# Weight pieces stored as they are loaded, with 4096-byte runs, and split by one operation of 1024 columns

## The chip, the cores and the metric

The kernel runs on one core of one Trainium2 chip. The metric is the device time of one execution in microseconds (us). A core has TensorE (matrix products, PE in the profile), VectorE (DVE), ScalarE (ACT), GpSimd (POOL) and SyncE (SP), each with its own instruction queue that is worked off in order, and 16 DMA engines that move data between HBM and the on-chip memory (SBUF) for whichever engine issued the transfer.

## The reference

One layer of a streaming encoder, for 1024 prompt rows and 64 sample rows that share the weights. All data are fp32, and D is 1024.

```python
xn = rmsnorm(x, g_mix)
p = xn @ w_in + b_in                      # 1024 -> 9224 columns: q, k, v, ig, fg, og, su, sv, xq, gates
h_a = sigmoid(og) * norm(mlstm(q, k, v, ig, log_sigmoid(fg)))
h_b = gelu(su) * (w_s @ rmsnorm(gelu(sv)) + b_s)
h_c = softmax(xq @ mem_k.T / 16) @ mem_v  # mem_k, mem_v = rmsnorm(mem) @ w_mk, w_mv
x = x + (g0 * h_a + g1 * h_b + g2 * h_c) @ w_out
# PEER: 8 heads, 128 x 128 product keys, the best 16 of 16384 experts for each row and head
q = rmsnorm(x, g_ffn) @ w_pq
e, g = top16(q @ k_sub1, q @ k_sub2)
x = x + sum_k g[k] * gelu(u_exp[e[k]] . xn) * v_exp[e[k]]
y = rmsnorm(x, g_final)
```

## The kernel before

The rows are nine tiles of up to 128 rows, in three blocks: [0, 1], [2, 3, 4, "s"] and [5, 6, 7]. "s" is the sample.

**Weights.** All dense weights pass through one stream of 560 pieces of 512 KB, each an SBUF tile of 128 partitions x 1024 columns. The list `pieces` holds them in the order of use: pieces 0 to 15 are w_mk and w_mv, then come 96 for each block (w_in, w_out, w_pq), and pieces 304 to 559 are the experts' matrices for the dense path. In DRAM a piece of a dense weight is two rows of 512 columns for each partition (runs of 2048 bytes), one of u_exp_t four rows of 256 columns (1024 bytes), one of v_exp two rows of 512 (2048 bytes). `w_load` issues a piece on SyncE into one of three buffers `wraw`; in the second phase every fourth piece goes to a further buffer, `wrawx`.

**Splits.** TensorE works in fp32r, and each weight is split in two parts: ScalarE casts a half of a piece (512 columns) to `wh` (line 277), and VectorE subtracts `wh` from it, which gives `wl` (line 280). For halves 192 to 223, GpSimd does the subtraction. Each half thus has its own pair of tiles, of which there are four (`HL`). The products with a half are the three terms xh*wh, xh*wl and xl*wh, in lines 311 to 313, 328 to 330, 1109 to 1111 and 1258 to 1260. The user of half i calls `w_get`, which first writes out the splits up to half i + 3, so the split of half i + 3 goes to the tiles of half i - 1 and waits until TensorE is done with those.

**Experts.** Tiles 0, 1, "s", 6 and 7 take their experts row by row: GpSimd issues an indirect DMA for each of 576 rows of u (tile `gu`, three buffers) and 576 rows of v (`gv`, four buffers), each of 128 x 4096 bytes (line 1018). VectorE consumes a u gather in line 1031 (a dot product with the row) and a v gather in line 1039 (a weighted sum into `gacc` or `gx`), one instruction of 128 x 1024 each. A buffer is gathered into again when VectorE is done with it.

**Dense path.** Tiles 2 to 5 take all 16384 experts as dense products, from piece 304 on: `hidden` (gelu of x times u, two pieces for 256 experts), times the expert weights that were spread out to `gd` in DRAM, and `dense` (times v, two pieces for 256 experts). A half is used by 12 matrix products of 512 columns here. `weigh` makes the two parts of a product with a cast (line 1228) and a subtraction (line 1229) of 1024 columns.

**Order.** Several generators (the blocks, mLSTM, the side branches, retrieval, the choice of experts, the gathers, the dense path) yield estimated costs to `Flow`, which writes out next the one that is furthest behind. The program so written passes a scheduler that puts each engine's instructions in order by its own simulated times. An engine's queue is in order at run time, so a subtraction of a split that stands behind a gather's consumption on VectorE waits for that gather too.

## Time and profile before

| | |
|---|---|
| median of three runs | 3675.89 us (3674.61 to 3696.73) |
| the profiled execution | 3700.63 us, of which the span from the first to the last instruction is 3698.9 us |
| TensorE busy | 3280.4 us (89%), 15364 matrix products recorded |
| VectorE busy | 3102.7 us (84%) |
| ScalarE busy | 1367.2 us (37%) |
| GpSimd busy | 1721.0 us (47%) |
| DMA | 1024.78 MB, 277 GB/s on average |

Matrix products are pipelined, so that a busy TensorE says only that it always had one under way. GpSimd's busy time is that of issuing the gathers and of a few operations. A wait is put down to the instruction that released it last.

### The profile page before, as it was taken

Reading aid. Unit: us, or ns where it says so; the run is one execution under the profiler, and the core shown is the slowest. Engines: PE = TensorE matmul, PEld = TensorE weight load, DVE = VectorE, ACT = ScalarE, POOL = GpSimd, SP = SyncE. Lnnn points to the kernel's source line nnn. Section 1 sums busy time; section 2 is a strip of 40 time slices with the busy share of each in tenths; the row PEclk is TensorE's granted clock in tenths of the full one; section 3 lists DMA queues with packets and bytes.
Section 4 is the critical chain, followed back from the end, with each engine's and each line's share of the span. In section 5 each row is a group of like instructions: output and inputs, shape, how many; then the busy total and the mean of one; then the engine's idle time right before and its main releaser. Section 6 shows DMA issues by size and latency. Waiting matters only on the chain.

```text
span 3698.9 us, 46231 instructions
## 1 busy us (share of the span) xinstructions
PE 3280.4 (89%) x15364; PEld 2632.8 (71%) x15364; DVE 3102.7 (84%) x6492; ACT 1367.2 (37%) x2479; POOL 1721.0 (47%) x1208
## 2 busy tenths in 40 slices
PE   8999998889996595898939765998999999999998
PEld 7787876576675473776938664876678888888886
DVE  5556797768899999899998999887798888879984
ACT  5555533423333242333415653322233333333332
POOL 1001334447765775465333475444465555446540
PEclk9999999999998697998959767999999999999999
DMA  7556477788897887898867788888899999989982
GB/s 230 148 165 188 152 245 248 254 279 321 320 367 273 272 306 252 276 334 285 302 209 220 235 269 292 312 287 276 295 376 337 337 339 337 328 282 386 356 303 85
DMA packets 447436, 1024.78 MB, mean 277 GB/s; under 512 B 32182, under 2 KB 169566, under 8 KB 443100
## 3 DMA queue, kind: packets, MB, share of 16 engines
q0 software_dynamic: 166528, 604.58, 47.0%
q1 hardware_dynamic: 276828, 413.06, 33.6%
q10 hardware_dynamic: 3840, 4.20, 0.3%
q8 instruction: 120, 1.97, 0.2%
q14 instruction: 120, 0.98, 0.1%
HBM read 968.44 MB, written 53.26 MB: 276 GB/s over the span
## 4 chain that ended last, share of the span: by engine, by line
PE 46%; DVE 20%; issue 13%; DMA 11%; POOL 8%; ACT 1%; POOLq 0%; DVEq 0%; ACTq 0%; SPq 0%
DMA gu<-in_u_exp_dram,e 7%; POOL gu L1018 5%; PE po L1260 5%; PE po L1259 5%; PE po L1258 5%; PE ph L1109 4%; PE ph L1111 4%; PE ph L1110 4%; DVE gacc L1039 4%; DVE gu L1031 4%; PE acc L312 3%; PE acc L311 3%; PE acc L313 3%; DVE wl L280 2%; DMA gv<-in_v_exp_dram,e 2%
## 5 line engine op out<-in xcount | busy, mean ns | idle before, releaser
L1018 POOL DMA_INDIRECT gv<-in_v_exp_dram,e x522 | 842.1, 1613 | 671.9 <-DVE gacc L1039 294.9
L1018 POOL DMA_INDIRECT gu<-in_u_exp_dram,e x576 | 756.8, 1314 | 774.6 <-DVE gu L1031 491.2
L277 ACT CAST wh<-wraw 128x512 fp32r<-128x512 f32 x994 | 613.0, 622 | 1347.9 <-PE ph L1110 481.5
L1031 DVE SCALAR_TENSOR_TENSOR gu<-gu,gx 128x1024 f32<-128x1024 f32 x576 | 701.6, 1220 | 195.2 <-DMA gu<-in_u_exp_dram,e 192.7
L280 DVE TENSOR_TENSOR wl<-wraw,wh 128x512 fp32r<-128x512 f32 x962 | 655.0, 686 | 228.4 <-ACT wh L277 226.2
L1039 DVE SCALAR_TENSOR_TENSOR gacc<-gv,w,gacc 128x1024 f32<-128x1024 f32 x448 | 573.1, 1279 | 33.3 <-DMA gv<-in_v_exp_dram,e 32.8
L312 PE MATMUL acc<-wl,half 128*128 128x512 f32 (+1 forms) x1152 | 474.1, 412 | 4.1 <-DVE wl L280 4.1
L313 PE MATMUL acc<-wh,half 128*128 128x512 f32 (+1 forms) x1152 | 456.2, 402 | 0.0
L1258 PE MATMUL po<-wh,W 128*128 128x512 f32 x1024 | 403.2, 399 | 32.6 <-ACT W L1228 32.6
L1111 PE MATMUL ph<-dxh,wl 128*128 128x512 f32 x1024 | 403.0, 394 | 18.5 <-DVE wl L280 18.4
L311 PE MATMUL acc<-wh,half 128*128 128x512 f32 (+1 forms) x1152 | 412.0, 410 | 6.5 <-ACT uB L470 5.1
L1259 PE MATMUL po<-wl,W 128*128 128x512 f32 x1024 | 408.7, 399 | 7.9 <-DVE wl L280 7.8
L1260 PE MATMUL po<-wh,W 128*128 128x512 f32 x1024 | 407.6, 398 | 0.6 <-DVE W L1229 0.6
L1109 PE MATMUL ph<-dxh,wh 128*128 128x512 f32 x1024 | 401.5, 392 | 1.3 <-DVE dxl L1133 1.3
L1110 PE MATMUL ph<-dxl,wh 128*128 128x512 f32 x1024 | 400.9, 391 | 0.0
L328 PE MATMUL acc<-half,wh 128*128 128x256 f32 (+2 forms) x768 | 250.2, 346 | 17.8 <-ACT wh L277 13.1
L311 PEld LDWEIGHTS acc<-wh,half 128*128 128x128 f32 (+1 forms) x1152 | 210.3, 184 | 77.8 <-issue 15.1
L312 PEld LDWEIGHTS acc<-wl,half 128*128 128x128 f32 (+1 forms) x1152 | 211.7, 184 | 71.4 <-issue 12.5
L329 PE MATMUL acc<-half,wh 128*128 128x256 f32 (+2 forms) x768 | 258.9, 342 | 0.0
L1258 PEld LDWEIGHTS po<-wh,W 128*128 128x128 f32 x1024 | 194.0, 189 | 80.3 <-issue 33.7
L313 PEld LDWEIGHTS acc<-wh,half 128*128 128x128 f32 (+1 forms) x1152 | 210.7, 184 | 54.4 <-issue 1.9
L330 PE MATMUL acc<-half,wl 128*128 128x256 f32 (+2 forms) x768 | 228.4, 343 | 15.5 <-DVE wl L280 8.5
(446 smaller groups left out, 5062.1 us busy)
## 6 DMA issues: line engine op xcount, KB each, us to landing
wraw<-in_w_in_dram SPq DMA_DIRECT2D x216, 512.0 KB
wraw<-in_v_exp_dram SPq DMA_DIRECT2D x126, 512.0 KB
wraw<-in_u_exp_t_dram SPq DMA_DIRECT2D x67, 512.0 KB
gd<-sg SPq DMA_DIRECT2D x16, 2048.0 KB
g<-gd SPq DMA_DIRECT2D x32, 1024.0 KB
wrawx<-in_u_exp_t_dram SPq DMA_DIRECT2D x61, 512.0 KB
wraw<-in_w_pq_dram SPq DMA_DIRECT2D x48, 512.0 KB
wraw<-in_w_out_dram SPq DMA_DIRECT2D x24, 512.0 KB
```

The lines of the kernel that those rows point to most:

```text
L277: S.copy(h, t)
L280: E.tensor_tensor(l, t, h.bitcast(F32), op=ALU.subtract)
L311: T.matmul(ps[i], xh[:, cs], h, start=(k == 0), stop=False)
L312: T.matmul(ps[i], xh[:, cs], l, start=False, stop=False)
L313: T.matmul(ps[i], xl[:, cs], h, start=False, stop=(last and b is None))
L1018: G.indirect_dma_start(out=tl, out_offset=None, in_=src, in_offset=bass.IndirectOffsetOnAxis(ap=col, axis=0))
L1031: V.scalar_tensor_tensor(tl, tl, 1.0, xn, op0=ALU.mult, op1=ALU.mult, accum_out=av[:, j:j + 1])
L1039: V.scalar_tensor_tensor(x2, gt_.pop(op), st_v[t][1][:, j:j + 1], x2, op0=ALU.mult, op1=ALU.add)
L1111: T.matmul(o, l[:, cs], xh[:, k + kk, :], start=False, stop=(k + kk == KD - 1))
L1258: T.matmul(o, hi, h, start=(q == 0 and k == 0), stop=False)
L1259: T.matmul(o, hi, l, start=False, stop=False)
L1260: T.matmul(o, lo, h, start=False, stop=(q == GP - 1 and k == 1))
```

## The change

All dense weights are stored in DRAM as the pieces themselves: for each piece 128 partitions x 1024 columns, so that each partition's part is one run of 4096 bytes. The content of a piece in SBUF is what it was. The eight gate columns of w_in get an array of their own, with runs of 256 bytes in place of 32. Everything else in `_layout` stays.

`wh` and `wl` become tiles of 1024 columns, a whole piece, with two buffers each in place of four of 512: as many bytes as before. For pieces 0 to 119 a piece is still cast and subtracted in two operations of 512 columns; from piece 120 on (`W1`), it is one cast and one subtraction of 1024. `w_get` of half i writes out the splits up to piece i // 2 + 1. At the first half of piece p, both halves of piece p + 1 are split into the tiles of piece p - 1; at the second half nothing is written. Before, the first half of piece p + 1 was written one half earlier. The loads have the same number, size and buffers, and GpSimd takes the same pieces (96 to 111) in halves.

```diff
-    RAW, HL = 3, 4
+    RAW, HL = 3, 2
...
     def want(src, c0):
         for kp in range(4):
-            pieces.append(src[kp * 256:(kp + 1) * 256, c0:c0 + 512].rearrange("(k p) c -> p k c", p=128))
+            pieces.append(src[c0 // 512, kp])
...
     POOL = 192, 224
+    POOL = POOL[0] // 2, POOL[1] // 2
+    W1 = 120
...
-        SP.dma_start(t.rearrange("p (k c) -> p k c", k=src.shape[1]), src)
+        SP.dma_start(t, pieces[i])
...
     def w_split():
-        i = W["split"]
-        if i >= 2 * len(pieces):
+        p = W["split"]
+        if p >= len(pieces):
             return
-        p, kk = divmod(i, 2)
         while W["load"] <= p:
             w_load()
-        t = raw_t[p][:, kk * 512:(kk + 1) * 512]
-        h = wp.tile([128, 512], F32R, name="wh", bufs=HL)
-        l = wp.tile([128, 512], F32R, name="wl", bufs=HL)
-        S.copy(h, t)
-
-        E = G if POOL[0] <= i < POOL[1] else V
-        E.tensor_tensor(l, t, h.bitcast(F32), op=ALU.subtract)
-        split_t[i] = (h, l)
+        t = raw_t.pop(p)
+        h = wp.tile([128, D], F32R, name="wh", bufs=HL)
+        l = wp.tile([128, D], F32R, name="wl", bufs=HL)
+
+        E = G if POOL[0] <= p < POOL[1] else V
+
+        n = 512 if p < W1 else D
+        for c in range(0, D, n):
+            cs = slice(c, c + n)
+            S.copy(h[:, cs], t[:, cs])
+            E.tensor_tensor(l[:, cs], t[:, cs], h[:, cs].bitcast(F32), op=ALU.subtract)
+        for c in range(2):
+            split_t[2 * p + c] = h[:, c * 512:(c + 1) * 512], l[:, c * 512:(c + 1) * 512]
         W["split"] += 1
-        if kk == 1:
-            raw_t.pop(p)
-            w_load()
+        w_load()
...
     def w_get():
         i = W["got"]
-        while W["split"] <= min(i + HL - 1, 2 * len(pieces) - 1):
+        while W["split"] <= min(i // 2 + HL - 1, len(pieces) - 1):
             w_split()
...
-                pieces.append(a["u_exp_t"][r * 512:(r + 1) * 512, m * 256:(m + 1) * 256]
-                              .rearrange("(k p) e -> p k e", p=128))
+                pieces.append(a["u_exp_p"][m, r])
...
-            pieces.append(a["v_exp"][e0:e0 + 256, hf * 512:(hf + 1) * 512].rearrange("(k p) c -> p k c", p=128))
+            pieces.append(a["v_exp_p"][GP * g + q, hf])
...
+    def parts(m):
+
+        return c(m.reshape(4, 2, 128, -1, 512).transpose(3, 0, 2, 1, 4).reshape(-1, 4, 128, 1024))
```

The scheduler orders each engine's instructions anew. Three places on VectorE show what came of it. The first is where the splits change their size, pieces 121 and 122, while the experts of the first block are chosen (`oh`, `ei` are tiles of that choice). Before:

```order
L280 TENSOR_TENSOR wl<-wraw,wh 128x512
L883 SCALAR_TENSOR_TENSOR xy<-pq__4542,xy 128x128
L889 SCALAR_TENSOR_TENSOR oh<-xy,ib 128x256 x4
L280 TENSOR_TENSOR wl<-wraw,wh 128x512
L892 TENSOR_TENSOR oh<-oh 128x512
L894 TENSOR_TENSOR ei<-oh 128x256
```

Now:

```order
L284 TENSOR_TENSOR wl<-wraw,wh 128x1024
L894 TENSOR_TENSOR oh<-oh 128x512
L896 TENSOR_TENSOR ei<-oh 128x256
L891 SCALAR_TENSOR_TENSOR oh<-xy,ib 128x256 x4
L647 COPY gt<-ms 128x12
```

What stood between the two subtractions of a piece now stands behind the one. The second place is in the third block, pieces 263 and 264, where VectorE consumes gathers of u and v, chooses experts (`scv`, `pos`, `tk`) and splits. Before:

```order
L280 TENSOR_TENSOR wl<-wraw,wh 128x512 x2
L1031 SCALAR_TENSOR_TENSOR gu,av<-gu,gx 128x1024
L1039 SCALAR_TENSOR_TENSOR gacc<-gv,w_17058,gacc 128x1024
L199 TENSOR_SCALAR rs<-rs 128x4
L1031 SCALAR_TENSOR_TENSOR gu,av<-gu,gx 128x1024
L800 MAX_INDEX pos<-scv,cand 128x8
L801 MATCH_REPLACE tk<-scv,cand 128x54
```

Now:

```order
L284 TENSOR_TENSOR wl<-wraw,wh 128x1024
L1033 SCALAR_TENSOR_TENSOR gu,av<-gu,gx 128x1024
L1041 SCALAR_TENSOR_TENSOR gacc<-gv,w_16042,gacc 128x1024
L879 TENSOR_TENSOR xy<-pq__11704 128x128
L874 SCALAR_TENSOR_TENSOR pq__11704<-pq__11704 128x128
L877 SCALAR_TENSOR_TENSOR pq__11704<-pq__11704 128x128
L883 TENSOR_TENSOR xy<-pq__11704 128x128
L1033 SCALAR_TENSOR_TENSOR gu,av<-gu,gx 128x1024
```

The gathers stand alike about a piece here, and the choice of experts has come further by this piece (`xy` is a later step of it than `pos`). Counted over VectorE's whole order, 524 of the 1152 gathers are consumed ahead of the end of piece 304's split before, and 536 now; ahead of piece 320's, 638 and 642; of piece 384's, 777 and 786. The third place is on the dense path, pieces 431 and 432, where VectorE has little but splits and gathers left (`ge` is the product with the expert weights). Before:

```order
L280 TENSOR_TENSOR wl<-wraw,wh 128x512
L1039 SCALAR_TENSOR_TENSOR gacc<-gv,w_24766,gacc 128x1024
L280 TENSOR_TENSOR wl<-wraw,wh 128x512
L1031 SCALAR_TENSOR_TENSOR gu,av<-gu,gx 128x1024
L1093 TENSOR_TENSOR ge<-ge,g_23951 128x1024
L1039 SCALAR_TENSOR_TENSOR gacc<-gv,w_24766,gacc 128x1024
```

Now:

```order
L284 TENSOR_TENSOR wl<-wraw,wh 128x1024
L1095 TENSOR_TENSOR ge<-ge,g_22495 128x1024
L1041 SCALAR_TENSOR_TENSOR gacc<-gv,w_23238,gacc 128x1024
L1033 SCALAR_TENSOR_TENSOR gu,av<-gu,gx 128x1024
L1041 SCALAR_TENSOR_TENSOR gacc<-gv,w_23238,gacc 128x1024
```

A piece had one to three other instructions behind each half's subtraction, and has all of them in a row behind the whole piece's.

## Rows read from the trace of the kernel before

**Rows 1.** The view of stretches, seven of them from the first to the last instruction: microseconds, then the busy time of TensorE (PE), its weight loads (PEld), VectorE (DVE), ScalarE (ACT) and GpSimd (POOL) with the number of instructions, the granted share of TensorE's clock, the busy share of the 16 DMA engines, and GB/s.

```profile
0.00:470.00 470.00, 444.89 (x2359) 367.95 (x2360) 283.13 (x825) 262.37 (x501) 51.99 (x55) 0.99 0.57 175
470.00:1100.00 630.00, 582.10 (x2486) 418.20 (x2486) 518.31 (x1086) 215.03 (x443) 355.81 (x246) 0.96 0.85 291
1100.00:1900.00 800.00, 616.09 (x2798) 504.70 (x2796) 760.59 (x2192) 271.88 (x520) 446.01 (x301) 0.86 0.84 284
1900.00:2400.00 500.00, 379.17 (x2333) 327.90 (x2334) 469.33 (x1003) 230.49 (x436) 266.28 (x130) 0.80 0.80 260
2400.00:2700.00 300.00, 274.62 (x1137) 214.37 (x1136) 228.88 (x355) 81.05 (x121) 128.04 (x107) 0.98 0.85 290
2700.00:3590.00 890.00, 888.95 (x3854) 723.96 (x3853) 791.00 (x959) 276.84 (x406) 472.87 (x371) 1.00 0.95 342
3590.00:3698.00 108.00, 94.55 (x405) 75.68 (x403) 51.42 (x80) 29.58 (x53) 0.00 (x0) 0.96 0.29 100
```

**Rows 2.** The waits of VectorE in three stretches, 470 to 1100 (two rows), 2400 to 2700 (one) and 2700 to 3590 (two): total microseconds, times, longest.

```profile
DVE gu L1031 <- DMA gu<-in_u_exp_dram,e: 92.2, 67, 5.9
DVE gacc L1039 <- DMA gv<-in_v_exp_dram,e: 14.0, 8, 3.8
...
DVE gu L1031 <- DMA gu<-in_u_exp_dram,e: 69.0, 45, 5.3
...
DVE wl L280 <- ACT wh L277: 71.8, 93, 2.0
DVE gu L1031 <- DMA gu<-in_u_exp_dram,e: 10.7, 8, 2.6
```

**Rows 3.** The waits of TensorE from 1100 to 1900 (two rows), 2400 to 2700 (two) and 2700 to 3590 (one), columns as in rows 2.

```profile
PE ms L819 <- ACT sc L822: 67.3, 8, 16.4
PE ms L733 <- DVE bb L720: 23.6, 2, 18.3
...
PE ph L1111 <- DVE wl L280: 18.4, 16, 2.7
PE po L1259 <- DVE wl L280: 6.8, 8, 2.2
...
PE po L1259 <- DVE wl L280: 1.0, 1, 1.0
```

**Rows 4.** Groups of instructions by line and shape, in the stretches 470 to 1100 (one row), 1100 to 1900 (two), 1900 to 2400 (two), 2400 to 2700 (three) and 2700 to 3590 (four): out<-in, shapes, count, busy microseconds, mean nanoseconds of one, and the idle time in front of them with what ended it. L280 is the subtraction of a split and L277 its cast; L1229 and L1228 are a subtraction and a cast of 1024 columns that the kernel does elsewhere; L1039 and L1031 consume a gather.

```profile
L280 DVE TENSOR_TENSOR wl<-wraw,wh 128x512 fp32r<-128x512 f32 x160 | 108.5, 683 | 2.0 <-ACT wh L277 1.8
...
L1039 DVE SCALAR_TENSOR_TENSOR gacc<-gv,w,gacc 128x1024 f32<-128x1024 f32 x161 | 205.3, 1275 | 10.9 <-DMA gv<-in_v_exp_dram,e 10.8
L280 DVE TENSOR_TENSOR wl<-wraw,wh 128x512 fp32r<-128x512 f32 x212 | 141.9, 681 | 12.3 <-ACT wh L277 12.2
...
L280 DVE TENSOR_TENSOR wl<-wraw,wh 128x512 fp32r<-128x512 f32 x46 | 31.4, 686 | 1.9 <-ACT wh L277 1.9
L280 DVE TENSOR_TENSOR wl<-wrawx,wh 128x512 fp32r<-128x512 f32 x15 | 10.2, 690 | 0.7 <-ACT wh L277 0.7
...
L1031 DVE SCALAR_TENSOR_TENSOR gu<-gu,gx 128x1024 f32<-128x1024 f32 x104 | 127.0, 1224 | 70.7 <-DMA gu<-in_u_exp_dram,e 69.0 <-DMA gx<-xn2d 1.4
L280 DVE TENSOR_TENSOR wl<-wraw,wh 128x512 fp32r<-128x512 f32 x71 | 48.6, 689 | 0.0
L280 DVE TENSOR_TENSOR wl<-wrawx,wh 128x512 fp32r<-128x512 f32 x24 | 16.5, 689 | 0.0
...
L280 DVE TENSOR_TENSOR wl<-wraw,wh 128x512 fp32r<-128x512 f32 x241 | 165.5, 690 | 68.7 <-ACT wh L277 68.1
L280 DVE TENSOR_TENSOR wl<-wrawx,wh 128x512 fp32r<-128x512 f32 x82 | 56.4, 687 | 3.9 <-ACT wh L277 3.8
L1229 DVE TENSOR_TENSOR W<-ge,W 128x1024 fp32r<-128x1024 f32 x40 | 48.9, 1222 | 6.3 <-ACT W L1228 6.0
L1228 ACT CAST W<-ge 128x1024 fp32r<-128x1024 f32 x40 | 42.0, 1050 | 74.2 <-PE po L1260 64.0 <-DVE ge L1093 10.1
```

**Rows 5.** The timeline of VectorE about 2577: start, duration, line, operation.

```profile
2576.45 0.69 DVE L280 TENSOR_TENSOR wl<-wraw,wh 128x512 fp32r<-128x512 f32 x1
2577.06 1.22 DVE L1093 TENSOR_TENSOR ge<-ge,g 128x1024 f32<-128x1024 f32 x1
2578.19 1.22 DVE L1031 SCALAR_TENSOR_TENSOR gu<-gu,gx 128x1024 f32<-128x1024 f32 x1
2579.34 0.08 DVE L1031 DVE_READ_ACCUMULATOR gu<-gu,gx 128x1 f32 x1
2579.34 0.69 DVE L280 TENSOR_TENSOR wl<-wrawx,wh 128x512 fp32r<-128x512 f32 x1
```

**Rows 6.** The timeline of ScalarE about 2967: start, duration, line, operation, and in brackets the idle time in front and what ended it.

```profile
2965.06 0.62 ACT L277 CAST wh<-wrawx 128x512 fp32r<-128x512 f32 x1 [1.49 <-PE po L1260]
2967.87 0.62 ACT L277 CAST wh<-wrawx 128x512 fp32r<-128x512 f32 x1 [2.19 <-PE po L1260]
2970.68 0.62 ACT L277 CAST wh<-wraw 128x512 fp32r<-128x512 f32 x1 [2.19 <-PE po L1260]
```

**Rows 7.** The DMA view: packets, megabytes and time as a share of 16 engines' span for the queue of the gathers (q0) and that of the loads issued by SyncE (q1); then one row of gathers, with the median time in microseconds from issue to landing at the end.

```profile
q0 software_dynamic: 166528, 604.58, 47.0%
q1 hardware_dynamic: 276828, 413.06, 33.6%
gu<-in_u_exp_dram,e POOLq DMA_INDIRECT x576, 6.4
```

More of the change, by code (lines that the diff above doesn't have):

```diff
@@ L146, in tile_stream_step @@
     wg_raw = mp.tile([128, KD, 8], F32, name="wg_raw", tag="sA")
-    G.dma_start(wg_raw, a["w_in"][:, O_IG:O_IG + 8].rearrange("(k p) c -> p k c", p=128))
+    G.dma_start(wg_raw, a["w_gate"])
     wgh = mp.tile([128, 2, KD, 4], F32R, name="wgh")
@@ L256, in w_load @@
             return
-        src = pieces[i]
         if now["dp"] is None or i % (RAW + 1):
@@ L571, in want_block @@
                   O_XQ, O_XQ + 512, O_OG, O_OG + 512, O_GT, O_GT + 512, O_GT + 2 * D, O_GT + 2 * D + 512):
-            want(a["w_in"], c)
+            want(a["w_in_p"], c - (8 if c > O_FG else 0))
         for c in (0, 512):
-            want(a["w_out"], c)
+            want(a["w_out_p"], c)
         for c in (0, 512, 1024, 1536):
-            want(a["w_pq"], c)
+            want(a["w_pq_p"], c)
     def main():
@@ L592, in tile_stream_step @@
         for c in (0, 512):
-            want(a[nm], c)
+            want(a[nm + "_p"], c)
     for _ in BLOCKS:
@@ L615, in tile_stream_step @@
             hf, q = divmod(j, GP)
-            e0 = (GP * g + q) * 256
-            pieces.append(a["v_exp"][e0:e0 + 256, hf * 512:(hf + 1) * 512].rearrange("(k p) c -> p k c", p=128))
+            pieces.append(a["v_exp_p"][GP * g + q, hf])
     def mlstm():
@@ L1311, in _layout @@
     d["g_mem_t"] = c(g["g_mem"][0].reshape(8, 128).T)
-    d["w_in"] = c(g["w_in"][0])
+    w = g["w_in"][0]
+    d["w_gate"] = c(w[:, O_IG:O_IG + 8].reshape(8, 128, 8).transpose(1, 0, 2))
+    def parts(m):
+        return c(m.reshape(4, 2, 128, -1, 512).transpose(3, 0, 2, 1, 4).reshape(-1, 4, 128, 1024))
+    d["w_in_p"] = parts(np.concatenate([w[:, 0:O_IG], w[:, O_OG:]], axis=1))
     d["b_in"] = c(b)
@@ L1325, in _layout @@
     d["b_s_t"] = c(bs)
-    d["w_mk"] = c(g["w_mk"][0])
-    d["w_mv"] = c(g["w_mv"][0])
-    d["w_out"] = c(g["w_out"][0])
-    d["w_pq"] = c(g["w_pq"][0])
+    d["w_mk_p"] = parts(g["w_mk"][0])
+    d["w_mv_p"] = parts(g["w_mv"][0])
+    d["w_out_p"] = parts(g["w_out"][0])
+    d["w_pq_p"] = parts(g["w_pq"][0])
     d["k_sub_t"] = c(np.stack([g["k_sub1"][0].T, g["k_sub2"][0].T], axis=1))
@@ L1332, in _layout @@
     d["v_exp"] = c(g["v_exp"][0])
-    d["u_exp_t"] = c(g["u_exp"][0].T)
+    d["u_exp_p"] = c(g["u_exp"][0].reshape(64, 256, 2, 4, 128).transpose(0, 2, 4, 3, 1).reshape(64, 2, 128, 1024))
+    d["v_exp_p"] = c(g["v_exp"][0].reshape(64, 2, 128, 2, 512).transpose(0, 3, 2, 1, 4).reshape(64, 2, 128, 1024))
     return d
```

## Prediction

> **What bounds the kernel now.** I read the view of stretches first, then who waits for whom in each stretch, then the durations of the two operations that are merged. No engine bounds the whole. Up to 470 us TensorE is busy for 445 of 470 us, and pieces 0 to 119 lie there. From 470 to 1100 no engine is full [rows 1]; VectorE stands for 92 + 14 us waiting for gathers to land [rows 2], with three u buffers that are refilled only after it has consumed them. From 1100 to 2400 VectorE is busy for 761 of 800 and 469 of 500 us and TensorE for 616 and 379 [rows 1], and TensorE waits there for what comes behind VectorE's queue (67 and 24 us) [rows 3]. From 2400 to 2700 VectorE waits 69 us for u gathers [rows 2], and TensorE stands 18 + 7 us because `wl` is queued behind those waits [rows 3]. From 2700 to 3590 TensorE is full (889 of 890 us) [rows 1], and VectorE waits for it: 72 us in front of subtractions, whose cast waits for TensorE to free a half [rows 2, 6]. The rest is the dense path's end.
>
> So a shorter VectorE queue is worth its time from 1100 to 2400, part of it in the two stretches that gathers pace, and nothing from 2700 on.
>
> **Merged splits.** Two subtractions of 512 columns last 2 x 0.69 us and one of 1024 lasts 1.22 [rows 4], a saving of 0.15 us a pair. But durations overlap when instructions stand back to back: a subtraction of 512 is followed after 0.61 us and one operation of 1024 after 1.13 [rows 5], which leaves 2 x 0.61 - 1.13 = 0.09 us. From 1100 to 2400 there are 212 + 46 + 15 halves [rows 4], 136 pairs: 12 us at 0.09, 20 at 0.15. As VectorE is nearly full there, the back-to-back value is nearer: -12. From 470 to 1100 and 2400 to 2700 there are 160 + 71 + 24 halves, 127 pairs [rows 4], 11 us at 0.09 and 19 at 0.15; as VectorE waits for gathers there, the gain may only lengthen a wait. Half of the 11: -6, between 0 and -19. The casts save 2 x 0.62 - 1.05 = 0.19 us a pair on ScalarE [rows 4, 6], which is busy for at most 46% of any stretch from 470 on [rows 1]: nothing.
>
> [...]
>
> **Run length.** The gathers, whose packets are mostly 4096 bytes, take 47.0% of the engines' span for 604.58 MB, and SyncE's queue takes 33.6% for 413.06 MB [rows 7]: 0.0777 and 0.0813% per MB. If all 560 pieces (294 MB) went over to the gathers' rate, they would save 294 x 0.0036 = 1.06% of the span, 39 us of the 16 engines' time. That counts only where transfers are waited for, 930 of 3699 us: 10 us at most. I take half of it, as the gap of 4% is partly due to other short transfers: -5, between 0 and -10. SyncE issues as many transfers as before.
>
> **The new order.** VectorE consumes 4 gathers more ahead of piece 320, at 1.28 us each [rows 4]: +5. Between pieces 320 and 384 it consumes 5 more, and 104 u gathers take the 300 us from 2400 to 2700 [rows 4], 2.9 us each. Some of the 5 fall where TensorE is full; I take three: +8. What is taken early is missing later, where TensorE is full, so that nothing comes back. If both are hidden it is 0, if none is 5 + 14: +13, between 0 and +19.
>
> **Less ahead.** A half takes TensorE 2.8 us on the dense path (the casts that wait for it are 2.81 us apart) [rows 6]. Before, a split had three halves, 8.4 us, between the freeing of its tiles and its use, for 0.62 + 0.69 us of work [rows 4, 6]: VectorE could come 7.1 us late. Now a piece has two halves, 5.6 us, for 1.05 + 1.22 us [rows 4]: 3.3 us late. From 2700 to 3590 VectorE's other work is 791 - 166 - 56 = 569 us [rows 1, 4] for 161 pieces (241 + 82 halves [rows 4]), 3.5 us a piece; with the split 4.7 of 5.6 us. On average that is enough, so the wait is hidden by TensorE's work; without that cover each late microsecond counts in full. Ahead of 470 us the same cover shrinks too, but nearly half of VectorE's time is free there [rows 1]. I take +5 for both places, between 0 and the price of the second rival.
>
> **The sum.** -12 - 6 - 5 + 13 + 5 = -5 us on the profiled execution's 3700.6, that is 3696. That execution is 25 us above the median of the runs, 3675.9, which goes by the same terms to 3671. I predict **3670 us**: no change that counts. A measurement of this kernel can tell about 1% from no change, so the bounds are 3639 and 3713.
>
> **Rivals.**
> *Gathers land sooner.* The loads' queue has 276,828 packets [rows 7]; the change takes 104,448 away (128 a piece in place of 256, and of 512 for 128 pieces). If that many turns on the engines delay the gathers, the 175 us for which VectorE waits for them from 470 to 1100 and 2400 to 2700 [rows 2] shrink by a third: 60 us, 3616. For it: a gather takes 6.4 us to land [rows 7], over four times the 1.5 us that it costs the engines (47.0% of 3699 us over 1152 gathers). Against it: time per byte differs by 4% only. It decides from a landing of about 5.8 us on.
> *TensorE waits for the splits.* This is the one that ends slower. It starts where VectorE comes over 3.3 us late to a split. A sum into `ob` (two operations of 1.2 us) falls on it every eighth piece, 20 times from 2700 to 3590; with a gather's wait of up to 2.6 us [rows 2] the lateness passes the 3.3. If each of the 20 costs the 2.4 us of its sums, it is 48 us: 3724. For it: TensorE waited for `wl` even with 7.1 us of cover from 2400 to 2700 [rows 3]. Against it: VectorE waits for TensorE for 72 us later [rows 2], so it is early most times.
> [...]
> [...] No row here shows how the two queues share an engine.
>
> **Chances.** No change that counts 0.55 (with the case in which every term is hidden); gathers sooner 0.25, which covers all outcomes faster by over 1%; TensorE waiting 0.13 and crowding 0.07, together slower by over 1%. The terms' own bounds give -20 - 19 - 10 = -49 to +19 without the second rival: 3627 to 3695, the likeliest case's range. For 8 in 10 I go to just past the faster rival, 3610, and past the slower one's 48 us, 3730.
>
> **What would show it.** One subtraction of 1024 columns in 1.22 us and one cast in 1.05; VectorE busy for some 60 us less (440 x 0.15). Gathers land in 6.3 to 6.5 us. From 2700 to 3590 TensorE stays full and its wait for `wl` stays under 10 us; 30 or more is the second rival. [...] I am wrong in the mechanism if the stretch from 1100 to 2400, where VectorE is full, changes by more than 30 us, or if the first 470 us grow by more than 5.

## Result and the profile after

The changed kernel takes 3732.8 us (median of four runs, 3730.6 to 3735.2), the kernel before 3681.9 in the same comparison: a ratio of 1.0133, 95% interval 1.0097 to 1.0169. It is slower by 1.3%, clear of the noise, and above both limits that the prediction set, 3713 and the wider 3730. The profiled execution took 3733.4 us with a span of 3731.6 us, 33 us more than that of before. (The profiled execution of before was itself longer than the median of its runs, so the profiles show 33 us of a loss of some 50.)

The stretches of [rows 1] again, in the kernel after (same columns):

```profile
0.00:470.00 470.00, 445.08 (x2385) 369.92 (x2386) 280.03 (x842) 255.61 (x504) 51.43 (x55) 1.00 0.56 176
...
1100.00:1900.00 800.00, 606.37 (x2739) 489.13 (x2737) 746.82 (x2011) 246.60 (x403) 468.61 (x306) 0.87 0.84 284
1900.00:2400.00 500.00, 365.74 (x2255) 317.18 (x2256) 462.45 (x1016) 220.71 (x402) 247.33 (x121) 0.75 0.77 248
2400.00:2700.00 300.00, 268.25 (x1103) 212.33 (x1103) 221.64 (x300) 69.38 (x70) 142.60 (x107) 0.97 0.83 288
2700.00:3590.00 890.00, 885.68 (x3830) 720.72 (x3829) 777.22 (x795) 245.91 (x244) 541.90 (x372) 1.00 0.93 340
```

TensorE is as full as before from 2700 on. It is less busy in each of the three stretches from 1100 to 2700, so the time was lost there.

The groups of the split in the kernel after, answering to [rows 4] (1100 to 1900 first, then 2700 to 3590), and its DMA rows, answering to [rows 7]:

```profile
L284 DVE TENSOR_TENSOR wl<-wraw,wh 128x1024 fp32r<-128x1024 f32 x105 | 126.8, 1209 | 4.2 <-ACT wh L283 4.2
...
L283 ACT CAST wh<-wraw 128x1024 fp32r<-128x1024 f32 x120 | 126.3, 1052 | 459.1 <-PE ph L1112 330.8 <-PE po L1262 122.9 <-issue 5.3
```

```profile
q0 software_dynamic: 166528, 604.58, 46.4%
q1 hardware_dynamic: 172380, 413.06, 32.8%
...
gu<-in_u_exp_dram,e POOLq DMA_INDIRECT x576, 6.1
```

One subtraction lasts 1.21 us and one cast 1.05, the loads' queue has 104,448 packets fewer, and a gather lands in 6.1 us. VectorE's busy time falls from 3102.7 to 3067.5 us, 0.08 us for each of the 440 merged pieces.

The waits of TensorE in the kernel after, from 1100 to 1900 (three rows), 2400 to 2700 (two) and 2700 to 3590 (one), answering to [rows 3]:

```profile
PE ms L735 <- DVE bb L722: 38.3, 2, 28.7
PE acc L315 <- DVE wl L284: 21.0, 11, 4.0
...
PE acc L333 <- DVE wl L284: 13.4, 7, 5.5
...
PE ph L1113 <- DVE wl L284: 24.1, 13, 4.4
PE po L1261 <- DVE wl L284: 7.7, 5, 2.2
...
PE ph L1113 <- DVE wl L284: 3.6, 3, 1.8
```

From 1100 to 1900 TensorE waits 34 us for `wl`. Before, it waited 9.5 us there, nearly all of it in this row:

```profile
PE acc L330 <- DVE wl L280: 8.5, 4, 3.8
```

Over the whole execution these waits add up to 39 us before and 95 us after.

A fixed window holds different work in the two kernels. To compare like with like I take the time at which the split of a piece ends: the rows of its subtraction in the timelines of VectorE (and of GpSimd for pieces 96 to 111) are counted, and the end of the last one of a piece is start plus duration. Piece 208 is split at 1158 us before and at 1139 after, piece 248 at 1534 and 1566, piece 320 at 2312 and 2321, piece 352 at 2499 and 2530, the last piece at 3675 and 3708. Step by step: -19 us up to piece 208, **+50 from 208 to 248**, -22 to 320, **+22 from 320 to 352**, +3 to the end. These are single executions: kernels with the same order of gathers (before and layout_only below, after and split_only) differ by up to 9 us in one step. The first three steps in part cancel, as the kernel after consumes 5 gathers fewer up to piece 208, 17 more up to 248 and 8 fewer up to 320. At piece 320 it is 9 us behind, at 352 31 us.

Two places lose. The stretches view for the first, before (1158 to 1534) and after (1139 to 1566), with the waits of VectorE for u gathers in each and, after, of TensorE for `wl`:

```profile
1158.00:1534.00 376.00, 264.25 (x1127) 206.28 (x1127) 357.18 (x1097) 124.06 (x244) 239.47 (x154) 0.80 0.81 276
DVE gu L1031 <- DMA gu<-in_u_exp_dram,e: 12.9, 16, 1.9
```

```profile
1139.00:1566.00 427.00, 275.86 (x1154) 208.99 (x1153) 382.14 (x1102) 123.48 (x212) 272.57 (x177) 0.81 0.82 271
DVE gu L1033 <- DMA gu<-in_u_exp_dram,e: 40.7, 24, 5.1
...
PE acc L315 <- DVE wl L284: 16.9, 7, 4.0
```

VectorE is busy for 25 us more and waits 28 us longer for gathers. Between these pieces 170 gathers are consumed in place of 153 (counted over its order); 17 at 1.22 to 1.28 us are some 21 of the 25. The second place, before (2312 to 2499) and after (2321 to 2530), with the waits of both engines:

```profile
2312.00:2499.00 187.00, 183.64 (x791) 147.99 (x790) 160.38 (x314) 59.86 (x87) 86.11 (x64) 1.00 0.87 300
DVE gu L1031 <- DMA gu<-in_u_exp_dram,e: 26.1, 18, 4.3
PE ph L1111 <- DVE wl L280: 3.2, 4, 1.4
```

```profile
2321.00:2530.00 209.00, 187.34 (x774) 148.03 (x773) 162.10 (x275) 51.64 (x51) 99.68 (x73) 0.97 0.83 286
DVE gu L1033 <- DMA gu<-in_u_exp_dram,e: 44.9, 29, 7.3
...
PE ph L1113 <- DVE wl L284: 16.3, 9, 7.2
PE po L1261 <- DVE wl L284: 4.9, 3, 2.2
```

Before, VectorE waited 26 us for gathers here and TensorE hardly noticed. After, 45 us become 21 us at TensorE. How one of them gets through stands in VectorE's timeline of the kernel after (start, duration, line, operation, idle time in front) and TensorE's:

```profile
2319.62 1.20 DVE L284 TENSOR_TENSOR wl<-wrawx,wh 128x1024 fp32r<-128x1024 f32 x1
...
2330.34 1.23 DVE L1033 SCALAR_TENSOR_TENSOR gu<-gu,gx 128x1024 f32<-128x1024 f32 x1 [7.34 <-DMA gu<-in_u_exp_dram,e]
...
2331.86 1.20 DVE L1271 TENSOR_TENSOR ob<-ob,po 128x1024 f32<-128x1024 f32 x1
2332.98 1.22 DVE L1033 SCALAR_TENSOR_TENSOR gu<-gu,gx 128x1024 f32<-128x1024 f32 x1
...
2334.39 1.20 DVE L284 TENSOR_TENSOR wl<-wraw,wh 128x1024 fp32r<-128x1024 f32 x1
```

```profile
2327.84 0.39 PE L1111 MATMUL ph<-dxh,wh 128*128 128x512 f32 x1
2328.06 0.39 PE L1112 MATMUL ph<-dxl,wh 128*128 128x512 f32 x1
2335.65 0.79 PE L1113 MATMUL ph<-dxh,wl 128*128 128x512 f32 x1 [7.19 <-DVE wl L284]
```

VectorE stands 7.3 us for one gather. The consumption of that gather, a sum into `ob`, the consumption of a second gather and some short operations come ahead of the next split in its queue, which begins 14.8 us after the last one. TensorE, which had two whole pieces at most, stands for 7.2 us.

### The profile page after: what moved, and what is told of

Its sections match the earlier page's. It is cut to its first block, busy times and chain, and to the rows that moved or that the text cites. A ratio compares the mean times of both kernels' runs of the same rounds, so it can differ in the third digit from the quotient of the medians.

```text
span 3731.6 us, 44746 instructions
## 1 busy us (share of the span) xinstructions
PE 3287.9 (88%) x15364; PEld 2633.4 (71%) x15364; DVE 3067.5 (82%) x6052; ACT 1280.9 (34%) x2039; POOL 1797.6 (48%) x1208
## 3 DMA queue, kind: packets, MB, share of 16 engines
q1 hardware_dynamic: 172380, 413.06, 32.8%
## 4 chain that ended last, share of the span: by engine, by line
PE 47%; DVE 21%; issue 13%; DMA 11%; POOL 7%; ACT 1%; POOLq 0%; DVEq 0%; SPq 0%; ACTq 0%
DMA gu<-in_u_exp_dram,e 8%; POOL gu L1020 6%; DVE gacc L1041 4%; PE ph L1113 4%; PE ph L1111 4%; PE ph L1112 4%; PE po L1261 4%; PE po L1262 4%; PE po L1260 4%; PE acc L314 4%; PE acc L315 4%; PE acc L316 4%; DVE gu L1033 3%; DVE wl L284 2%; PE acc L333 1%
## 5 line engine op out<-in xcount | busy, mean ns | idle before, releaser
L1020 POOL DMA_INDIRECT gu<-in_u_exp_dram,e x576 | 810.1, 1406 | 752.3 <-DVE gu L1033 442.4
L1020 POOL DMA_INDIRECT gv<-in_v_exp_dram,e x522 | 856.7, 1641 | 635.9 <-DVE gacc L1041 299.7
L283 ACT CAST wh<-wraw 128x1024 fp32r<-128x1024 f32 (+1 forms) x617 | 532.9, 883 | 1341.4 <-PE ph L1112 516.5
L284 DVE TENSOR_TENSOR wl<-wraw,wh 128x1024 fp32r<-128x1024 f32 (+1 forms) x585 | 594.3, 1029 | 222.4 <-ACT wh L283 221.3
L316 PE MATMUL acc<-wh,half 128*128 128x512 f32 (+1 forms) x1152 | 461.0, 406 | 0.7 <-DVE half L229 0.7
L314 PE MATMUL acc<-wh,half 128*128 128x512 f32 (+1 forms) x1152 | 422.7, 416 | 9.4 <-ACT wh L283 6.8
L1260 PE MATMUL po<-wh,W 128*128 128x512 f32 x1024 | 386.6, 397 | 31.6 <-ACT W L1230 31.1
L1262 PE MATMUL po<-wh,W 128*128 128x512 f32 x1024 | 408.4, 399 | 0.6 <-DVE W L1231 0.6
L1113 PEld LDWEIGHTS ph<-dxh,wl 128*128 128x128 f32 x1024 | 195.5, 191 | 85.9 <-DVE wl L284 45.1
L331 PE MATMUL acc<-half,wh 128*128 128x256 f32 (+2 forms) x768 | 247.1, 341 | 7.2 <-ACT wh L283 3.3
L332 PE MATMUL acc<-half,wh 128*128 128x256 f32 (+2 forms) x768 | 253.2, 338 | 0.0
```

Source lines behind the costliest of these rows:

```text
L284: E.tensor_tensor(l[:, cs], t[:, cs], h[:, cs].bitcast(F32), op=ALU.subtract)
L314: T.matmul(ps[i], xh[:, cs], h, start=(k == 0), stop=False)
L316: T.matmul(ps[i], xl[:, cs], h, start=False, stop=(last and b is None))
L1020: G.indirect_dma_start(out=tl, out_offset=None, in_=src, in_offset=bass.IndirectOffsetOnAxis(ap=col, axis=0))
L1113: T.matmul(o, l[:, cs], xh[:, k + kk, :], start=False, stop=(k + kk == KD - 1))
L1260: T.matmul(o, hi, h, start=(q == 0 and k == 0), stop=False)
```

## Experiments

From the traces I had one theory and three rivals. *Order*: the scheduler places more gathers ahead of the splits (424 in place of 412 ahead of piece 248, 710 in place of 701 ahead of 352). *Run length*: the longer runs hold up the gathers or other transfers. *The merged operation*: an operation of 1024 columns costs time by itself. *Look-ahead*: two whole-piece tiles hold less work for TensorE than four half tiles, so that a split that stands behind a gather is felt. How late a split may come before TensorE stands still is called its cover here. All kernels give their ratio to the kernel before. The table under the last experiment has every piece time.

### 1. Parts of the change

layout_only is the change without the split: the code of before for `w_split` and `w_get`, `HL = 4`, tiles of 512 columns.

> The DRAM layout of after alone: whole pieces in runs of 4096 bytes, but the splits of before (two of 512 columns, four half tiles ahead). The order of instructions on VectorE is then that of before, with 524 gathers consumed ahead of piece 304's split and 638 ahead of piece 320's. The theory of the order (the loss comes from more gathers consumed early, 524 to 536 and 638 to 642, where VectorE and the gathers set the pace) expects before's time, 3670 to 3685 us. The rival of the run length (the longer runs hold up the gathers or the other transfers) expects after's time, 3725 to 3735 us, with gathers that land later than after's.

Measured: ratio 1.0020 (1.0000 to 1.0041). It has the order of before, and its time but for some 7 us. The loads' queue takes 32.8% of the span as in after, and a u gather lands in 6.5 us. The longer runs neither make the loss nor bring anything.

split_only is the change without the layout: the sources of before (`src[kp * 256:(kp + 1) * 256, c0:c0 + 512]` and its like) with the splits of after.

> The splits of after alone (whole-piece tiles two ahead, one operation of 1024 columns from piece 120 on), with the weights laid out as before. The order of instructions on VectorE is that of after (536 gathers ahead of piece 304, 642 ahead of piece 320). The theory of the order expects after's time, 3725 to 3740 us. The rival of the run length expects before's time, 3670 to 3685 us.

Measured: 1.0130 (1.0082 to 1.0178), all of the loss. It lies in the split.

```diff
-    W1 = 120
+    W1 = 560
```

> After with the bound for merging at 560, so that every piece is still split in two operations of 512 columns, but into the whole-piece tiles of after, two of them ahead. Gathers consumed ahead of a split: 313 at piece 216 (before 318, after 319), 413 at 248 (412, 424), 525 at 304 (524, 536), 639 at 320 (638, 642), 706 at 352 (701, 710), 782 at 384 (777, 786). The theory of the order expects the loss between pieces 208 and 248 nearly gone, as 157 gathers stand there against 153 of before and 170 of after, and half of that between 320 and 352 kept: 3685 to 3705 us in all. The rival of the shorter look-ahead (two whole tiles hold up the splits more than four half ones) expects after's time, 3725 to 3740. The rival of the merged operation itself expects before's, 3670 to 3685.

Measured: 1.0118 (1.0085 to 1.0151). Here nothing is merged, and the loss is there. The theory of the order was wrong on this kernel: 157 gathers stand between pieces 208 and 248, near the 153 of before, and that stretch still takes 398 us against 376. The rival of the merged operation falls, that of the look-ahead stands: this kernel has nearly the order of layout_only and takes 1.0% longer, and TensorE waits 76 us for `wl` in place of 46.

```diff
-    W1 = 120
+    W1 = 304
```

> After with the merge only from piece 304 on, that is on the dense path alone; ahead of it the splits are of 512 columns in whole-piece tiles. Gathers consumed ahead of a split: 525 at piece 304 (before 524, after 536), 634 at 320 (638, 642), 705 at 352 (701, 710). The theory of the order expects no loss between 208 and 248 and, with 71 gathers between 320 and 352 against 63 of before and 68 of after, the full loss of some 20 us there: 3690 to 3705 us. The rival of the shorter look-ahead expects 3725 to 3740. The rival of the merged operation itself expects the loss on the dense path alone, behind piece 320, some 20 us, and none ahead.

Measured: 1.0127 (1.0092 to 1.0161), with 398 us between 208 and 248 where nothing is merged. Again the look-ahead's number, not the order's.

```diff
-    RAW, HL = 3, 4
+    RAW, HL = 3, 3
```

The edit above is made to layout_only.

> The layout of after with the splits of before in half tiles, but three half tiles of wh and wl in place of four: a shorter look-ahead with nothing else of the change. Gathers consumed ahead of a split are then 422 at piece 248 (before 412, after 424), 533 at 304 (524, 536), 639 at 320 (638, 642), 705 at 352 (701, 710). If the look-ahead of the tiles is what sets the order (a split that must wait for a tile lets gathers pass), and the order or the missing cover makes the loss, the time is that of after, 3720 to 3745 us. If it is the whole-piece tile as such, or the operation of 1024 columns, the time is that of before, 3680 to 3700 us.

Measured: 1.0140 (1.0104 to 1.0176). One half tile less, with no whole-piece tile and no merge, costs as much as the whole change, and its gathers come forward (422 ahead of 248, 533 ahead of 304). That does not make the look-ahead the source of after's order. unmerged has the tiles of after and before's counts (413 and 525), and the same edit in three_two below leaves them near there too (413 and 527). The merge has a part in after's 424, since unmerged differs from after in that alone. Why the scheduler lets gathers pass in the one kernel and not in the other is not shown.

### 2. The order by itself

The next two part the order from the tiles. The first changes layout_only:

```diff
-            yield 2.5 if now["dp"] is None else 2.2
+            yield 1.55 if now["dp"] is None else 2.2
```

> The layout of after with the splits of before (two of 512 columns, four half tiles ahead), and one number changed: the gathers' stream asks for its turn after 1.55 in place of 2.5 in the first part, so that the order brings the gathers forward as in after. Consumed ahead of a split: 344 at piece 224 (before 335, after 342), 362 at 232 (354, 363), 420 at 248 (412, 424), 530 at 304 (524, 536), 643 at 320 (638, 642), 708 at 352 (701, 710). The theory of the order (the place of the gathers on VectorE by itself makes the loss, whatever the tiles) expects after's time, 3715 to 3735 us, with the loss between pieces 208 and 248. The rival of the cover (four half tiles let TensorE run on while a split waits behind a gather, two whole ones don't) expects 3680 to 3700 us.

Measured: 1.0103 (1.0069 to 1.0137). With four half tiles the early gathers alone cost 0.8% over layout_only, some 30 us: 397 us between 208 and 248 (layout_only 382), 782 to 320 (768), 204 to 352 (190). The order does cost time without the tiles: the 3727.9 us are what the theory of the order expected, and the rival of the cover was wrong with 3680 to 3700. But the loss was expected between 208 and 248, and it lies in three steps, 14 or 15 us in each. TensorE waits 60 us for `wl` here, 46 in layout_only.

The second holds gathers back in after, with edges that set only the order of issue (`split_ins[p]` is the subtraction of piece p):

```diff
+PINS = [
+    (318, 215), (335, 223), (354, 231), (368, 239), (412, 247),
+]
...
-            consume(ops[s_])
+            behind = [p for g, p in PINS if g <= s_ and p in split_ins]
+            if behind:
+                with tc.issue_after(split_ins[behind[-1]]):
+                    consume(ops[s_])
+            else:
+                consume(ops[s_])
```

> After, with five fixed points in VectorE's order: no gather from the 318th on is consumed ahead of piece 215's split, none from the 335th ahead of 223's, from the 354th ahead of 231's, from the 368th ahead of 239's and from the 412th ahead of 247's, which are the counts of before. From piece 207's split to 247's that leaves 148 gathers (after 170, before 153); what is held is made up by piece 304 (532 against 536), and the rest is as after. The theory of the order expects the stretch between the splits of pieces 208 and 248, 376 us before and 427 after, back at 375 to 390 us, a part of it given back between 248 and 304, and 3700 to 3720 us in all. The rival of the cover (whole-piece tiles, two ahead) expects that stretch to stay above 410 us and the time at 3725 to 3740 us.

Measured: 1.0126 (1.0091 to 1.0162), 3737.4 us, the time that the rival of the cover expected. The stretch from 208 to 248 came down from 426 to 397 us with 148 gathers, between what the two theories expected, and from 248 to 320 it gave nearly the same back (781 us against after's 755). So more than half of the 50 us goes with the gathers, and the rest stays with whole-piece tiles. Here a held gather was only paid for later, ahead of piece 352.

### 3. Gathers moved to where TensorE is full

Now the edges hold gathers until TensorE is full. before_held puts `PINS = [(305, 215), (340, 239), (390, 247), (510, 303)]` into the kernel before.

> The kernel before with four fixed points in VectorE's order and nothing else: no gather from the 305th on is consumed ahead of piece 215's split, none from the 340th ahead of 239's, from the 390th ahead of 247's and from the 510th ahead of 303's. Consumed ahead of a split: 386 at piece 248 (before 412), 489 at 304 (524), 624 at 320 (638), 691 at 352 (701), 1135 at 544 (1146). If each gather consumed ahead of piece 352 costs its 2.6 us, and none behind it, the time is some 26 us below before's, 3650 to 3665. If a held gather is only paid for in another place, it is before's, 3680 to 3695. If those held are missing at the end, where 17 are left at piece 544 in place of 6, it is 3690 or more.

Measured: 0.9964 (0.9939 to 0.9988), 3673.0 us: 13 us of the 26, and in none of the three ranges.

> The kernel before with the four fixed points of before_held set 15 to 20 gathers lower (the 290th, 325th, 375th and 490th). Consumed ahead of a split: 367 at piece 248 (before 412), 473 at 304 (524), 606 at 320 (638), 681 at 352 (701), 1119 at 544 (1146). By 2.6 us for each of the 20 fewer ahead of piece 352 the time is some 52 us below before's, 3625 to 3645. If a held gather is only paid for in another place, it is before's, 3680 to 3695. If those held are missing at the end, it is above before_held's.

Measured: 0.9917 (0.9887 to 0.9947), 3652.8 us: 31 of the 52 us, and above the range. Nothing is missing at the end.

before_one has `PINS = [(638, 319)]`.

> The kernel before with one fixed point: no gather from the 638th on is consumed ahead of piece 319's split. The order is that of before up to piece 312; then 603 gathers are consumed ahead of 320 (before 638), 680 ahead of 352 (701) and 1118 ahead of 544 (1146). By 2.6 us for each of the 21 fewer ahead of piece 352 the time is some 55 us below before's, 3625 to 3645. If only the count between pieces 320 and 352 matters, 77 in place of 63, the loss is that of after there and more, 20 to 40 us, and what is saved ahead of 320 is nothing, since other work sets the pace there: 3700 to 3725.

Measured: 0.9874 (0.9824 to 0.9924), 3636.5 us, as the count ahead of 352 had it. The rival is wrong, since from 320 to 352 it consumes 77 gathers in 174 us, where before took 187 us for 63.

after_held is after with the four points of before_held.

> After with the four fixed points of before_held. Consumed ahead of a split: 368 at piece 248 (after 424), 477 at 304 (536), 609 at 320 (642), 693 at 352 (710), 1137 at 544 (1152). By 2.6 us for each of the 17 fewer ahead of piece 352 the time is some 45 us below after's, 3680 to 3695, and the merged operation is then worth nothing against before. If the whole-piece tiles have a price of their own, it stays at 3710 or more. If a held gather is only paid for in another place, it stays at 3725 to 3740.

Measured: 1.0010 (0.9985 to 1.0035), 3689.1 us, some 44 below after's, where the count had 45. With the same points it is still 0.5% above before_held.

Up to here the count of gathers ahead of piece 352 seemed to carry the loss. The next two test it, with `PINS = [(630, 319), (670, 351)]` in before and in after.

> The kernel before with two fixed points: no gather from the 630th on ahead of piece 319's split, none from the 670th on ahead of piece 351's. The order is that of before up to piece 312; then 601 gathers are consumed ahead of 320 (before 638), 670 ahead of 352 (701), 743 ahead of 384 (777) and 1113 ahead of 544 (1146). The 21 fewer of before_one brought 49 us, 2.3 each; by that the 31 fewer here bring 71: 3610 to 3630 us. If the end is then too full for what is held, where TensorE's pieces 384 to 448 took 358 us in before_one and 349 before, it is 3640 or more.

> After with the two fixed points of before_two. Consumed ahead of a split: 602 at piece 320 (after 642), 670 at 352 (710), 747 at 384 (786), 1118 at 544 (1152): from 320 on the counts of before_two; ahead of 304 after's own, 536 against 524. If the count ahead of piece 352 carries the whole loss, it equals before_two, 3610 to 3635 us. If whole-piece tiles have a price of their own, it is 10 to 25 us above before_two. If the loss is laid down between pieces 208 and 248 for good, it is 30 us or more above.

Measured: before_two 0.9822 (0.9792 to 0.9852), 3621.8 us; after_two 1.0000 (0.9982 to 1.0017), 3685.3 us. At the same counts from piece 320 on they are 63 us apart, so the count is not the whole cause. By their piece times 43 us of the difference are there at piece 248, 21 at 320 and 44 at 352: after_two loses 23 us between 320 and 352 with as many gathers, and 18 behind 352. Of its three expectations the one with 30 us or more came true, but not for its reason alone: part of the loss comes behind piece 320.

### 4. Order or cover at the same count

early_two gives gathers_early the points of before_two, so that half tiles have nearly the order of after_two all along. three_two gives before_two three half tiles.

```diff
-    RAW, HL = 3, 4
+    RAW, HL = 3, 3
```

> gathers_early (layout of after, half tiles four ahead, the turn of 1.55) with the two fixed points of before_two. Its counts of gathers ahead of a split are near those of after_two all along: 344 at piece 224 (after_two 342), 420 at 248 (424), 530 at 304 (536), 601 at 320 (602), 670 at 352 (670). If the cover is what whole-piece tiles lack, then only what the early gathers cost ahead of 304 is left: 16 us above before_two, and 6 for the layout, 3635 to 3650 us, with 176 to 182 us between the splits of pieces 320 and 352. If the order is the cause, it equals after_two, 3675 to 3690 us, with some 204 us there.

> before_two with three half tiles of wh and wl in place of four. Counts of gathers ahead of a split are near those of before_two: 336 at piece 224 (335), 413 at 248 (412), 527 at 304 (524), 604 at 320 (601), 670 at 352 (670). If the cover is the cause, it is 25 us or more above before_two, 3645 to 3685 us, with 190 to 205 us between the splits of pieces 320 and 352. If the order is the cause, it equals before_two, 3615 to 3635 us, with 176 to 182 us there.

Measured: early_two 0.9897 (0.9858 to 0.9937), 3643.7 us; three_two 0.9958 (0.9937 to 0.9979), 3668.2 us. Both times are what the cover expects; early_two's step from 320 to 352, 186 us, lies just above its 176 to 182. With after_two's order but four half tiles, 42 of the 63 us are gone. With nearly before_two's order but three half tiles, 46 us are lost. (These are differences of medians; by the ratios they are 38 and 50.) TensorE's waits for `wl` go the same way: 22 us in before_two, 38 in early_two, 80 in three_two and 85 in after_two. The stretch from 320 to 352 in before_two (2264 to 2445), early_two (2273 to 2459), three_two (2283 to 2478) and after_two (2285 to 2488), with the waits for u gathers on VectorE and for `wl` on TensorE:

```profile
2264.00:2445.00 181.00, 179.64 (x776) 145.36 (x776) 162.66 (x270) 58.37 (x84) 94.85 (x72) 1.00 0.91 319
DVE gu L1039 <- DMA gu<-in_u_exp_dram,e: 17.7, 18, 1.9
PE po L1272 <- DVE wl L286: 0.8, 1, 0.8
```

```profile
2273.00:2459.00 186.00, 182.54 (x788) 147.38 (x786) 162.76 (x270) 57.85 (x85) 93.05 (x71) 1.00 0.88 313
DVE gu L1037 <- DMA gu<-in_u_exp_dram,e: 22.0, 17, 3.5
...
PE ph L1122 <- DVE wl L285: 3.5, 3, 1.6
```

```profile
2283.00:2478.00 195.00, 184.54 (x764) 145.19 (x763) 159.13 (x254) 55.69 (x81) 87.26 (x67) 0.97 0.84 289
DVE wl L286 <- ACT wh L283: 18.2, 13, 2.1
DVE gu L1039 <- DMA gu<-in_u_exp_dram,e: 16.6, 16, 2.3
...
PE ph L1124 <- DVE wl L286: 7.6, 5, 5.2
```

```profile
2285.00:2488.00 203.00, 186.19 (x765) 147.18 (x764) 156.47 (x228) 50.17 (x49) 99.82 (x69) 0.96 0.80 276
DVE gu L1041 <- DMA gu<-in_u_exp_dram,e: 25.3, 15, 3.7
DVE wl L290 <- ACT wh L289: 20.1, 8, 4.4
...
PE ph L1126 <- DVE wl L290: 9.6, 6, 3.9
```

With four half tiles 18 to 22 us of waits for gathers leave TensorE 1 to 4 us of its own. With less, VectorE also stands 18 to 20 us in front of a subtraction whose cast waits for TensorE to free a tile. That the gathers behind it run late in turn is likely, but not shown by itself.

All piece times, from the profiled executions in us, gathers consumed ahead of the splits of pieces 248 and 352, and the sum of TensorE's waits for `wl` over the whole execution in us. (The counts are taken at the split one piece earlier than the times, which makes 2 to 6 gathers.)

| kernel | to 208 | 208-248 | 248-320 | 320-352 | 352-end | gathers ahead of 248, 352 | TensorE waits for `wl` |
|---|---|---|---|---|---|---|---|
| before | 1158 | 376 | 777 | 187 | 1176 | 412, 701 | 39 |
| layout_only | 1153 | 382 | 768 | 190 | 1175 | 412, 701 | 46 |
| after | 1139 | 426 | 755 | 209 | 1179 | 424, 710 | 95 |
| split_only | 1137 | 429 | 760 | 211 | 1171 | 424, 710 | 99 |
| unmerged | 1158 | 398 | 772 | 200 | 1178 | 413, 706 | 76 |
| merge_dense | 1149 | 398 | 770 | 198 | 1183 | 413, 705 | 76 |
| half_three | 1155 | 401 | 761 | 197 | 1182 | 422, 705 | 103 |
| gathers_early | 1154 | 397 | 782 | 204 | 1168 | 420, 708 | 60 |
| gathers_held | 1141 | 397 | 781 | 214 | 1183 | 402, 709 | 93 |
| before_held | 1151 | 359 | 789 | 172 | 1177 | 386, 691 | 37 |
| before_held3 | 1135 | 328 | 811 | 172 | 1169 | 367, 681 | 23 |
| before_one | 1141 | 380 | 744 | 174 | 1163 | 412, 680 | 26 |
| after_held | 1138 | 342 | 796 | 194 | 1186 | 368, 693 | 70 |
| before_two | 1139 | 386 | 740 | 181 | 1146 | 412, 670 | 22 |
| after_two | 1140 | 427 | 717 | 204 | 1164 | 424, 670 | 85 |
| early_two | 1143 | 395 | 735 | 186 | 1152 | 420, 670 | 38 |
| three_two | 1146 | 391 | 746 | 195 | 1160 | 413, 670 | 80 |

The eight kernels with four half tiles wait 22 to 60 us for `wl`, the nine with less 70 to 103.

## Why the prediction was wrong, step by step

**Less ahead: the step that failed.** It put the cover at 7.1 us before and 3.3 after, and then looked for the harm ahead of 470 us and from 2700 on alone, there at the average load of VectorE (4.7 of 5.6 us), and took +5 with up to 48 above it. From 2700 to 3590 TensorE's wait for `wl` is indeed 4 us. The cover is missed between 470 and 2700, where VectorE waits for gathers: 90 of the 95 us of TensorE's waits for `wl` lie there, 38 before. A wait of up to 7.3 us comes on top of what VectorE has to do, and no average tells of it. One half tile of cover is worth 46 us (three_two against before_two), and what after_two lacks beyond its order is 42 us with the merge's gain already taken off (after_two against early_two). The places differ by kernel: in after the loss stands out in two steps, in three_two it is 7, 5, 6, 14 and 14 us in the five. [Rows 2, 3] had it: 69 us of waits for gathers from 2400 to 2700 with 25 at TensorE, with the full cover.

**The new order: right in sign, mis-sized.** It was +13, at most +19. gathers_early has nearly that order with half tiles and costs 0.8% over layout_only, some 30 us (the two intervals leave some 15 to either side). I counted 9 gathers from the totals ahead of 320 and 384. Between 208 and 248 there are 17 more, and the totals hide them, since fewer stand elsewhere. That nothing comes back behind, because TensorE is full there, was right: gathers moved behind piece 352 bring time in before_one, before_two and after_held. The step also took the order as given apart from the splits, while half_three and unmerged show that tiles and merge both move it.

**Merged splits: right for VectorE, not for the time.** -18 in all was predicted, and after takes 3732.8 us and unmerged, which has the same tiles, 3728.9: nothing is left of the merge. By steps after is 19 us shorter than unmerged up to piece 208, but merge_dense, which merges nothing there either, is 9 us shorter too, so about half of it is within the spread. From 248 to 320 after is 17 us shorter with 8 gathers fewer, which alone could account for it, and from 208 to 248 28 us longer with 13 more. The merge's own gain can't be read from these steps, since the order changes with it. The sign that VectorE would be busy for some 60 us less (440 x 0.15) did not come either: it was 35, near the 40 that 0.09 a pair gives. Up to 470 us nothing grew, as expected.

**Run length: wrong in sign, small.** -5 was predicted; layout_only shows +0.2% (0 to 0.41%). The loads' share of the engines fell from 33.6% to 32.8% of the span, near the 1.06% worked out. VectorE's waits for gathers stayed about the same by it, 221 us in layout_only and 226 before. Gathers did not land as soon as the rival on them asked, by about 5.8 us: they land in 6.1 us in after and 6.5 in layout_only. The chance of 0.07 for crowding was the author's estimate, and no run shows how the queues of the loads and the gathers share an engine; what the runs show in its place is these two landings, against 6.4 us before, and the 0.2% of layout_only.

**The rival that ends slower was the mechanism, in another place.** It had TensorE waiting for splits that stand behind a gather's wait and a sum into `ob`, 3724 us, at 0.13. The timeline about 2330 shows just that, but ahead of 2700. The sum into `ob` is no needed part of it: 50 of the 95 us of waits for `wl` in after (the rows of `acc`) come ahead of the dense path, which alone has that sum. That its price, 48 us for 20 sums from 2700 on, comes near the measured loss is luck. Its chance was too low since I held VectorE's later waits for TensorE (72 us [rows 2]) against it, which belong to another stretch. The prediction's own sign of a wrong mechanism, the stretch from 1100 to 2400 changing by more than 30 us, is met: pieces 200 to 335, which before splits between 1099 and 2395 us, take 34 us more in after.

**Open.** How much of the 50 us between 208 and 248 is cover and how much is order was only parted roughly (gathers_held: 29 and 21, with 5 gathers fewer than before in the stretch). The two prices don't add up either: 30 us of order over layout_only and 42 of cover with the gathers held would be 72, and after is 41 above layout_only, so each price holds in the kernel in which it was measured. Three whole-piece tiles, which would keep the merge with the cover, were not tried. Why 77 gathers fit into 174 us in before_one is not settled. Its VectorE runs 259 instructions there against 314 before, so part of the other work had gone by.

## What to carry to other kernels

When two half tiles become one whole tile, count how late the producer may come at each place where its queue can stall, by the longest wait in that place and what queues behind it, not by the average load. Where a scheduler sets the order, a change of tiles or of the size of an operation can also move other work in front, and then cover and order both have a price; compare the orders before trusting the sum. Work that only has to be done sometime belongs where the bounding engine has no need of its engine: two fixed points that hold gathers back (before_two) brought 1.8%, where the change that saved instructions on the busy engine lost 1.3%.

## What the hardware showed that was not expected

Three of TensorE's waits cost more than their length. The stretches view of the kernel after about the wait of 7.2 us at 2328 (columns as in rows 1):

```profile
2325.00:2328.00 3.00, 3.00 (x15) 2.49 (x14) 0.00 (x0) 0.19 (x1) 0.00 (x0) 1.00 1.01 401
2328.00:2336.00 8.00, 0.81 (x3) 0.39 (x3) 5.66 (x18) 2.14 (x2) 2.47 (x2) 0.84 0.51 182
2336.00:2340.00 4.00, 4.00 (x10) 3.12 (x10) 4.00 (x18) 0.31 (x1) 2.21 (x2) 0.50 0.85 269
2340.00:2345.00 5.00, 5.00 (x22) 4.05 (x21) 4.52 (x13) 2.03 (x2) 1.88 (x2) 0.97 0.89 311
```

Behind the wait the granted clock is 0.50 until about 2340, and a matmul follows the last one after 0.43 us in place of 0.23. Counted over the starts of the matmuls, 24 of the 772 between pieces 320 and 352 are that slow in after, in three groups, each just behind a wait for `wl` (of 7.19, 2.25 and 1.96 us), and none of 789 before: another 24 x 0.2 = 5 us beside the 21 of the waits.

More gathers in less time did not make them land later for VectorE. From 320 to 352 (2265 to 2439) before_one moves more than before did there, and VectorE waits less for gathers, where before waited 26.1 us:

```profile
2265.00:2439.00 174.00, 174.00 (x754) 141.56 (x754) 167.27 (x259) 56.20 (x82) 102.49 (x76) 1.00 0.96 343
...
DVE gu L1039 <- DMA gu<-in_u_exp_dram,e: 2.0, 4, 1.2
```
